# In-chunk key by receptance products made once and kept in DRAM, receptance 0 projected ahead of key 1

## The chip, the cores and the metric

The kernel runs on one core of a Trainium2 chip. The metric is the device time of one launch in microseconds, the median of three runs. The engines are named as the profile names them: PE (TensorE, with PEld for its weight loads), DVE (VectorE), ACT (ScalarE), POOL (GpSimd) and SP (SyncE, which here only issues DMAs).

## The reference, cut to what matters

Two layers, each with four branches that are fed by one projection of the normalised input (1024 prompt tokens and 8 sequences of 16 new tokens, 1152 in all). The change lies in branch A, a recurrence over tokens with a matrix state `s` of 64 x 64 for each of four heads:

```
def step(s, inp):
    r_t, w_t, k_t, v_t, kk_t, a_t = inp
    sa = jnp.einsum('bhij,bhj->bhi', s, -kk_t)
    s = (s * w_t[:, :, None, :] + sa[:, :, :, None] * (kk_t * a_t)[:, :, None, :]
         + v_t[:, :, :, None] * k_t[:, :, None, :])
    return s, jnp.einsum('bhij,bhj->bhi', s, r_t)
```

`r` is called the receptance, `k` the key, `v` the value. The kernel computes it by chunks of 64 tokens: with the decays worked into keys and receptances, all that the tokens of a chunk do to each other is a masked product of keys by receptances, and the part of it that couples the removal keys is a unit-triangular system, which is inverted.

## The kernel before, in words

**Projections.** The input is projected in 24 tiles of 128 features a layer, in the order `F_ORDER` (L35): WDAD (decay and learning rate), K0 and K1 (keys of heads 0, 1 and 2, 3), R0 and R1 (receptances), V0 and V1 (values), then the tiles of the other branches (D0, GD0, D1, GD1, VC0, VC1, U0, GC0, U1, GC1 and so on). `project` (L238) runs a tile over three groups of 384 tokens; a group is 24 matmuls of 128 x 384 into one of two PSUM banks `pj`, and then a sink on ACT and DVE that empties the bank. WDAD and K0 run side by side, group after group. Weights come as pairs of k-tiles by SP, are split in two parts by ACT (L234) and GpSimd (L235), and are asked for two tiles ahead.

**Work beside the projections.** Generators wait in lanes; `tick` (L135) advances the head of each lane by one step. A projection ticks a few times within each group (for most tiles twice, and once more after the sink, so three times a group). Lane "a" is one queue and holds, in this order, `a_elem` for each key group (L417, elementwise work of a key group, five pieces), `systems` (L496), `solve` (L510) and `recurrence` (L699). The program order that comes out is a priority: a planner places the instructions of each engine, and each engine then runs its own list in order.

**Branch A.** `a_elem(i, g)` writes, for heads pair i and token group g, the tile `KB` (scaled removal keys and keys) and the first half of `AR` (scaled removal keys); `receptance(i, ..)` (L479) multiplies the receptances into the second half of `AR` on GpSimd (L482).
- `systems(g)` (L496): for each of the six chunks of a group four products of 64 by 64 (removal keys only) into one PSUM bank, a mask on DVE (L504) into `ns` (two buffers), and a store on ACT's queue (L505) into the DRAM tile `nd` (`nds` for chunks 16 and 17, the new tokens). Two chunks are one step.
- `solve` (L510): SP loads the diagonal blocks of all chunks (L518, L519), DVE inverts them one per partition (L528 and L530, 46 steps of two operations), ACT issues the stores of the inverses into `dd` and `dds` (L536 to L543).
- `prepare(c)` (L550), in three steps: SP loads the chunk's inverse `tt` (L561), four products of 128 by 128 with key and receptance columns, two DVE masks (L570) into `Gm` (tag `gm`, two buffers), transposes of keys and values; products that complete the inverse with the off-diagonal block; the product of `Gm` with the values (L626).
- `advance(c)` (L631), in three steps: `U` from the state and the inverse, the new state, the outputs (L689, which reads `Gm` last). `prepare` of the next chunk runs beside `advance`.
- `split`, `groupnorm` and the gates use the outputs later.

PSUM tiles `b` (four banks) hold the products of `systems`, `prepare` and `advance`. Large SBUF tiles `m` (eight buffers) hold projections, the inverses and the pooling branch's tiles. The order around the change stands at L895 to L922: `systems(g - 1)` is queued after K1's group g, `systems(2)` and `solve` with idle ticks between them after K1; R0, R1, V0, V1, D0 follow; `recurrence` is queued after D0 and runs beside GD0 to U0.

Of the kernel before, what the change touches and what calls it, by code (L numbers as in the profile page):

```python
# [10 lines left out]
F32 = mybir.dt.float32  # L11
# [19 lines left out]
# projection tiles, in the order in which they are streamed  # L31
# [3 lines left out]
F_ORDER = (WDAD, K0, K1, R0, R1, V0, V1, D0, GD0, D1, GD1, VC0, VC1, U0, GC0, U1, GC1,  # L35
           Q0, Q1K, CK, GB0, GB1, GA0, GA1)

# columns of the per-feature vectors
# [4 lines left out]
# constant matrices  # L43
# [5 lines left out]
def tile_trunk(ctx: ExitStack, tc: tile.TileContext, *aps):  # L49
# [34 lines left out]
    def split(src, by, view=lambda t: t):  # L84
        """two exact parts of a tile; by: engines of the copy and of the difference"""
# [9 lines left out]
    def total(out, m, parts, start=True, stop=True):  # L95
        """sums over partitions of a tile in two parts, weighted by small integers"""
        mm(out, m, parts[0], start, False)
        mm(out, m, parts[1], False, stop)
# [16 lines left out]
    # Work that runs beside the large products: lanes of generators, each advanced by one step per tick.  # L115
# [37 lines left out]
    # running input of the layer: 4 tiles of [128, 2, G] per token group, and sums of squares  # L153
# [15 lines left out]
    # sums over partitions: of all, of each half; of the halves of queries  # L169
# [21 lines left out]
    def raw_weights(fi, src):  # L191
        """a whole tile of weights ahead of its splitting"""
        raw[fi] = m_tile(1024).rearrange("p (k t) -> p k t", k=8)
        SY.dma_start(out=raw[fi], in_=src)
# [14 lines left out]
    def recip1p(t):  # L209
        """t <- 1 / (1 + t)"""  # L210
# [11 lines left out]
    def load_weights(n):  # L222
        """weights as two exact parts, in pairs of k-tiles in their order of use"""
# [14 lines left out]
    def project(keys, hi, lo, sinks, ticks=(3,)):  # L238
        """one tile of features, or several of them side by side, group after group of tokens"""
# [58 lines left out]
    # zero at the first token of each chunk (64 tokens; 16 in the last 128 columns)  # L298
# [11 lines left out]
    # rows of the chunks' inverses, zero off the diagonal blocks  # L310
    # (half chunks of 64 rows; the room behind each lets the diagonal blocks lie at equal distances)
# [3 lines left out]
    def whole(t, c, cols):  # L315
        """the two halves of chunk c"""
        return t[2 * c:2 * c + 2, 0:128 * cols].rearrange("x (s t) -> x s t", s=64)

    def diagonal(t, i, n, cols, first=0):
        """the n x n blocks of the halves' matrices: block b of rows at columns first + b n"""  # L320
# [14 lines left out]
    for l in range(L):  # L335
        last_layer = l == L - 1
# [22 lines left out]
        # ================= A: features with token shift =================  # L359
# [57 lines left out]
        def a_elem(i, g, k):  # L417
# [11 lines left out]
            # decay, learning rate, square sums of the removal key  # L429
# [29 lines left out]
            # normalised removal key  # L459
# [4 lines left out]
            # in-context learning rate  # L464
# [14 lines left out]
        def receptance(i, fr):  # L479
            def after(g, zs):  # L480
                ex = AR[i][g][:, :, 1, :]
                Po.tensor_tensor(out=ex, in0=chv(zs), in1=ex, op=ALU.mult)  # L482
            shifted(fr, lambda g: s_tile("gn", 3), after)
# [7 lines left out]
        nd, nds = halves(f"nd{l}", 32, 64), halves(f"nds{l}", 4, 64)  # L491

# [3 lines left out]
        def systems(g):  # L496
            for cl in range(6):
                c = 6 * g + cl
                pn = pb()[:, 0:128].rearrange("p (i t) -> p i t", i=2)
                for h in range(4):  # L500
                    mm(pn[hp(h), h // 2, :], KB[h // 2][g][hp(h), cl, h % 2, :], AR[h // 2][g][hp(h), cl, 0, :])
                ns = chp.tile([128, 2, 64], F32, tag="u0", name=nm("ns"), bufs=2)
                mk = cm[:, C_MP if c < 16 else C_MS, 0:64]
                V.tensor_tensor(out=ns, in0=pn, in1=mk.unsqueeze(1).broadcast_to([128, 2, 64]), op=ALU.mult)  # L504
                A.dma_start(out=whole(nd, c, 64) if c < 16 else whole(nds, c - 16, 64),  # L505
                            in_=ns.rearrange("p i t -> p (i t)"))
# [43 lines left out]
        def prepare(c):  # L550
            """what a chunk needs besides the state, in three steps"""
# [10 lines left out]
            # masked products of the chunk  # L562
            Gm = chp.tile([128, 2, 2, 128], F32, tag="gm", name=nm("gm"), bufs=2)
            for hh in range(2):
                pg = pb()[:, 0:256].rearrange("p (i t) -> p i t", i=2)
                pr = slice(64 * hh, 64 * hh + 64)
                for i in range(2):
                    mm(pg[:, i, :], KB[i][g][pr, cl].rearrange("p a t -> p (a t)"),
                       AR[i][g][pr, cl].rearrange("p a t -> p (a t)"))
                V.tensor_tensor(out=Gm[:, hh], in0=pg,  # L570
                                in1=cm[:, C_MS if samp else C_MP, :].unsqueeze(1).broadcast_to([128, 2, 128]),
                                op=ALU.mult)
            # token-major copies of keys and values
# [13 lines left out]
            # inverse of the chunk's unit-triangular system  # L587
# [965 lines left out]
```

## Time and profile before

| | us |
|---|---|
| three runs | 1474.29, 1471.72, 1472.41 |
| median | 1472.41 |
| span of the profiled execution | 1470.1 |
| PE busy in it | 1395.4 |
| DVE, ACT, POOL busy | 782.2, 751.9, 436.8 |

The profiled execution is one run; its span goes from the first to the last instruction. Busy time of an engine is the union of its instructions; PE's matmuls overlap each other, so a group's busy time is less than its count times the mean. A wait is put down to what came last by semaphores.

### The profile page before, as it was taken

How to read it: one execution, taken by the hardware profiler on the slowest of the kernel's cores; microseconds unless marked ns; L12 is line 12 of the kernel's file. 1: busy time of each engine (PE TensorE's matmuls, PEld its weight loads, DVE VectorE, ACT ScalarE, POOL GpSimd, SP SyncE). 2: the span in 40 equal slices, each digit the busy share in tenths (PEclk: the TensorE clock that was granted, in tenths of full speed). 3: DMA queues.
4: the chain of work that ended last, by engine and by line, in shares of the span. 5: the costliest groups of instructions: out<-in, count | busy, mean ns of one | idle time of the engine just before them, and what ended most of it. 6: DMA issues, size and time to landing. Idle time of an engine off the chain costs nothing. (4 is left out here: it accounts for less than half of the span.)

```text
span 1470.1 us, 26810 instructions
## 1 busy us (share of the span) xinstructions
PE 1395.4 (95%) x9938; PEld 1158.6 (79%) x9938; DVE 782.2 (53%) x1762; ACT 751.9 (51%) x2017; POOL 436.8 (30%) x575
## 2 busy tenths in 40 slices
PE   4898899999999999999979988999999999999999
PEld 3678778888987776689967787888899778666998
DVE  7985944445136457742387857433632464677211
ACT  6672244655366667642257522455644666666210
POOL 4514314346321110322262333332652111112320
PEclk9999999999999999999989999999999999999999
DMA  7113241111212114033300123221021111131232
GB/s 224 48 33 81 52 101 49 55 46 38 93 42 70 53 31 130 6 114 97 87 22 29 52 66 73 77 69 47 30 78 60 57 53 55 37 109 43 69 96 77
DMA packets 116594, 97.38 MB, mean 66 GB/s; under 512 B 46128, under 2 KB 111344, under 8 KB 116464
## 3 DMA queue, kind: packets, MB, share of 16 engines
q1 hardware_dynamic: 76776, 73.74, 17.1%
q10 hardware_dynamic: 39688, 21.94, 5.0%
q8 instruction: 78, 1.28, 0.4%
q14 instruction: 52, 0.43, 0.1%
HBM read 71.48 MB, written 24.16 MB: 65 GB/s over the span
## 5 line engine op out<-in xcount | busy, mean ns | idle before, releaser
L76 PE MATMUL pj<-xh,wh 128*128 128x384 f32 x1152 | 413.6, 360 | 18.5 <-ACT xh L273 7.3
L76 PE MATMUL pj<-xl,wh 128*128 128x384 f32 x1152 | 395.4, 343 | 4.1 <-POOL xl L275 3.1
L76 PE MATMUL pj<-xh,wl 128*128 128x384 f32 x1152 | 394.8, 343 | 0.0
L235 POOL TENSOR_TENSOR wl<-wr,wh 128x256 fp32r<-128x256 f32 x200 | 155.0, 783 | 484.3 <-ACT wh L234 421.9
L76 PEld LDWEIGHTS pj<-xh,wh 128*128 128x128 f32 x1152 | 220.2, 191 | 45.2 <-ACT sho L390 11.5
L76 PEld LDWEIGHTS pj<-xl,wh 128*128 128x128 f32 x1152 | 220.3, 191 | 11.8 <-POOL xl L275 5.5
L76 PEld LDWEIGHTS pj<-xh,wl 128*128 128x128 f32 x1152 | 220.0, 191 | 7.6 <-issue 6.4
L76 PE MATMUL pj<-yh,wh 128*128 128x384 f32 x384 | 130.0, 339 | 2.4 <-DVE x L1376 2.4
L76 PE MATMUL pj<-yh,wl 128*128 128x384 f32 x384 | 129.2, 336 | 0.0
L76 PE MATMUL pj<-yl,wh 128*128 128x384 f32 x384 | 129.0, 336 | 0.0
L234 ACT ACTIVATE wh<-wr 128x256 fp32r<-128x256 f32 x200 | 80.8, 414 | 93.9 <-PE pj L76 45.9
L76 PEld LDWEIGHTS pj<-yh,wh 128*128 128x128 f32 x384 | 72.5, 189 | 3.7 <-DVE x L1376 2.8
L235 POOL TENSOR_TENSOR wl<-m,wh 128x256 fp32r<-128x256 f32 x56 | 43.5, 787 | 102.2 <-ACT wh L234 75.8
L76 PEld LDWEIGHTS pj<-yh,wl 128*128 128x128 f32 x384 | 72.7, 189 | 0.1
L76 PEld LDWEIGHTS pj<-yl,wh 128*128 128x128 f32 x384 | 72.6, 189 | 0.1
L1251 ACT ACTIVATE X<-b,ng 128x512 f32<-128x512 f32 (+3 forms) x96 | 54.9, 575 | 28.8 <-DVE ng L1243 24.7
L76 PEld LDWEIGHTS st<-X,X 128*64 128x64 f32 x576 | 35.7, 136 | 31.7 <-DVE mx L1239 6.3
L76 PE MATMUL b<-sp,cr 128*128 128x384 f32 (+3 forms) x192 | 58.7, 386 | 1.0 <-POOL sp L92 0.6
L1239 DVE TENSOR_REDUCE mx<-b 128x1 f32<-128x512 f32 (+3 forms) x96 | 53.0, 552 | 8.3 <-PE b L76 6.9
L1372 DVE TENSOR_TENSOR pt<-pj,pt 128x384 f32<-128x384 f32 x24 | 13.4, 557 | 80.6 <-PE pj L76 80.6
L234 ACT ACTIVATE wh<-m 128x256 fp32r<-128x256 f32 x56 | 22.5, 413 | 62.0 <-PE pj L76 60.9
L76 PE MATMUL st<-X,X 128*64 128x128 f32 x576 | 53.6, 283 | 0.3
(295 smaller groups left out, 2556.9 us busy)
## 6 DMA issues: line engine op xcount, KB each, us to landing
wr<-in_win_dram SPq DMA_DIRECT2D x176, 128.0 KB
m<-in_wout_dram SPq DMA_DIRECT2D x12, 512.0 KB
x<-in_xT_dram SPq DMA_DIRECT2D x12, 384.0 KB
ysp<-m ACTq DMA_DIRECT2D x24, 192.0 KB
pt<-in_xT_dram SPq DMA_DIRECT2D x24, 192.0 KB
ea<-ysp SPq DMA_DIRECT2D x24, 192.0 KB
x1d<-x ACTq DMA_DIRECT2D x24, 192.0 KB
pt<-x1d SPq DMA_DIRECT2D x24, 192.0 KB
```

Of the source, the lines that this page charges most:

```text
L76: PE.matmul(out, lhsT=lhsT, rhs=rhs, start=start, stop=stop, skip_group_check=True)
L234: A.activation(out=h, in_=r, func=AF.Copy)
L235: Po.tensor_tensor(out=lo, in0=r, in1=h.bitcast(F32), op=ALU.subtract)
L1239: V.tensor_reduce(out=mx[:, b:b + 1], in_=pc[:, :w], axis=AX.X, op=ALU.max)
L1251: A.activation(out=P[:, :w], in_=pc[:, :w], func=AF.Exp, scale=SCALE, bias=ng, accum_out=sums[pr][:, b, s, h:h + 1])
L1372: V.tensor_tensor(out=xr, in0=ps, in1=xr, op=ALU.add)
```

## The change

`F_ORDER` gets R0 between K0 and K1, and the order of the calls follows. `systems(g)` is queued after the receptance of group g of R1 has been multiplied in, makes the four products of 128 by 128 that `prepare` made, masks them into `Gm` (tag `gm`, two buffers), stores the removal-key half to `nd` in two pieces on SP's queue and the whole `Gm` to a new DRAM tile `gd` on ACT's queue. `prepare` loads `Gm` from `gd` on SP's queue in place of products and masks. `solve` follows after two idle ticks.

```diff
-F_ORDER = (WDAD, K0, K1, R0, R1, V0, V1, D0, ...
+F_ORDER = (WDAD, K0, R0, K1, R1, V0, V1, D0, ...
...
         def receptance(i, fr):
             def after(g, zs):
                 ex = AR[i][g][:, :, 1, :]
                 Po.tensor_tensor(out=ex, in0=chv(zs), in1=ex, op=ALU.mult)
+                if i == 1:
+                    go("a", systems(g))
...
         nd, nds = halves(f"nd{l}", 32, 64), halves(f"nds{l}", 4, 64)
+        gd = dr.tile([18, 128, 512], F32, tag=f"gd{l}", name=nm("gd"))
...
         def systems(g):
             for cl in range(6):
                 c = 6 * g + cl
-                pn = pb()[:, 0:128].rearrange("p (i t) -> p i t", i=2)
-                for h in range(4):
-                    mm(pn[hp(h), h // 2, :], KB[h // 2][g][hp(h), cl, h % 2, :], AR[h // 2][g][hp(h), cl, 0, :])
-                ns = chp.tile([128, 2, 64], F32, tag="u0", name=nm("ns"), bufs=2)
-                mk = cm[:, C_MP if c < 16 else C_MS, 0:64]
-                V.tensor_tensor(out=ns, in0=pn, in1=mk.unsqueeze(1).broadcast_to([128, 2, 64]), op=ALU.mult)
-                A.dma_start(out=whole(nd, c, 64) if c < 16 else whole(nds, c - 16, 64),
-                            in_=ns.rearrange("p i t -> p (i t)"))
+                samp = c >= 16
+                pg = [pb()[:, 0:256].rearrange("p (i t) -> p i t", i=2) for _ in range(2)]
+                for i in range(2):
+                    for hh in range(2):
+                        pr = slice(64 * hh, 64 * hh + 64)
+                        mm(pg[hh][:, i, :], KB[i][g][pr, cl].rearrange("p a t -> p (a t)"),
+                           AR[i][g][pr, cl].rearrange("p a t -> p (a t)"))
+                Gm = chp.tile([128, 2, 2, 128], F32, tag="gm", name=nm("gm"), bufs=2)
+                mk = cm[:, C_MS if samp else C_MP, :]
+                for hh in range(2):
+                    V.tensor_tensor(out=Gm[:, hh], in0=pg[hh], in1=mk.unsqueeze(1).broadcast_to([128, 2, 128]),
+                                    op=ALU.mult)
+                for hh in range(2):
+                    half = nds[2 * (c - 16) + hh] if samp else nd[2 * c + hh]
+                    SY.dma_start(out=half[0:128 * 64].rearrange("(s i t) -> s i t", s=64, i=2),
+                                 in_=Gm[64 * hh:64 * hh + 64, hh, :, 0:64])
+                A.dma_start(out=gd[c], in_=Gm.rearrange("p h i t -> p (h i t)"))
                 if cl % 2:
                     yield
...
         def prepare(c):
...
             Gm = chp.tile([128, 2, 2, 128], F32, tag="gm", name=nm("gm"), bufs=2)
-            for hh in range(2):
-                pg = pb()[:, 0:256].rearrange("p (i t) -> p i t", i=2)
-                pr = slice(64 * hh, 64 * hh + 64)
-                for i in range(2):
-                    mm(pg[:, i, :], KB[i][g][pr, cl].rearrange("p a t -> p (a t)"),
-                       AR[i][g][pr, cl].rearrange("p a t -> p (a t)"))
-                V.tensor_tensor(out=Gm[:, hh], in0=pg,
-                                in1=cm[:, C_MS if samp else C_MP, :].unsqueeze(1).broadcast_to([128, 2, 128]),
-                                op=ALU.mult)
+            SY.dma_start(out=Gm.rearrange("p h i t -> p (h i t)"), in_=gd[c])
...
         def after_k1(g, zs):
             start("a", a_elem(1, g, zs))
-            if g > 0:
-                go("a", systems(g - 1))
...
+        receptance(0, R0)
         shifted(K1, lambda g: zk1[:, gcols(g)], after_k1)
-        go("a", idle(4))
-        go("a", systems(2))
-        go("a", idle(4))
+        receptance(1, R1)
+        go("a", idle(2))
         go("a", solve())
-        receptance(0, R0)
-        receptance(1, R1)
         values(V0)
```

## Rows read from the trace of the kernel before

**Rows 1.** The page, part 1: busy us, share of the span, instructions.
```profile
PE 1395.4 (95%) x9938; PEld 1158.6 (79%) x9938; DVE 782.2 (53%) x1762; ACT 751.9 (51%) x2017; POOL 436.8 (30%) x575
```
**Rows 2.** Busy time by stretch: from:to, length, engines, granted clock, DMA share, GB/s.
```profile
97.00:133.00 36.00, 32.60 (x255) 28.28 (x256) 21.58 (x51) 11.95 (x32) 11.84 (x16) 1.00 0.20 56
141.90:186.70 44.80, 39.34 (x273) 36.86 (x272) 42.00 (x118) 9.43 (x28) 16.94 (x24) 0.95 0.22 56
...
205.00:347.00 142.00, 139.63 (x1612) 116.69 (x1611) 62.97 (x144) 80.59 (x278) 59.50 (x75) 1.00 0.18 55
...
38.00:97.00 59.00, 51.71 (x249) 39.55 (x248) 52.68 (x90) 43.94 (x109) 22.53 (x26) 0.96 0.13 37
```
**Rows 3.** Timeline of DVE, masks of `systems`: start, us, what, idle before.
```profile
97.41 0.28 DVE L504 TENSOR_TENSOR ns<-b,cm 128x128 f32<-128x128 f32 x1
...
123.10 0.29 DVE L504 TENSOR_TENSOR ns<-b,cm 128x128 f32<-128x128 f32 x1 [1.58 <-DMA nd<-ns]
...
132.25 0.29 DVE L504 TENSOR_TENSOR ns<-b,cm 128x128 f32<-128x128 f32 x1 [1.53 <-DMA nd<-ns]
```
**Rows 4.** Waits of PE: waited for, us in total, times, longest.
```profile
PE b L76 <- DVE gm L570: 5.9, 3, 2.9
PE b L76 <- DVE ns L504: 5.0, 4, 1.4
```
**Rows 5.** Groups by line and form: shapes, count, busy us, mean ns, idle before.
```profile
L570 DVE TENSOR_TENSOR gm<-b,cm 128x256 f32<-128x256 f32 x72 | 28.3, 417 | 6.7 <-PE b L76 6.7
L76 PE MATMUL b<-ar,kb 64*128 64x128 f32 x288 | 27.0, 302 | 0.0
...
L76 PE MATMUL b<-ar,kb 64*64 64x64 f32 x288 | 15.3, 228 | 5.9 <-DVE ns L504 5.0 <-DVE kb L471 0.8
...
L504 DVE TENSOR_TENSOR ns<-b,cm 128x128 f32<-128x128 f32 x36 | 10.4, 288 | 24.6 <-DMA nd<-ns 21.8 <-PE pj L76 2.3
```
**Rows 6.** Busy time by stretch, as rows 2: stores of `nd`, `dd`, `ysp`.
```profile
121.50:125.50 4.00, 2.71 (x40) 2.13 (x38) 0.61 (x3) 0.00 (x0) 0.77 (x1) 1.00 0.13 36
...
186.90:194.90 8.00, 7.05 (x48) 5.91 (x47) 1.20 (x4) 3.00 (x8) 0.00 (x0) 0.84 0.89 132
196.80:197.40 0.60, 0.60 (x6) 0.60 (x5) 0.60 (x4) 0.48 (x3) 0.01 (x1) 1.00 0.77 277
```
**Rows 7.** Timelines of ACT and SP: two stores and the next issue awaiting each.
```profile
1396.54 0.34 ACTq L1373 DMA_DIRECT2D out_yT_dram<-pt  x1
...
1398.45 0.32 SPq L1370 DMA_DIRECT2D pt<-x1d  x1
...
371.90 0.33 ACTq L891 DMA_DIRECT2D ysp<-m  x1
...
374.73 0.33 SPq L929 DMA_DIRECT2D m<-in_wukv_dram  x1
```
**Rows 8.** The chain that ended last, where projection groups follow each other: start, us.
```profile
1089.32 16.91 PE pj L76 x96
```
**Rows 9.** Timeline of GpSimd: the receptance multiply of R1's first group.
```profile
118.13 1.01 POOL L482 TENSOR_TENSOR ar<-gn,ar 128x384 f32<-128x384 f32 x1 [2.29 <-DVE gn L387]
```
**Rows 10.** Timelines of SP and DVE: a load of the solve, the inversion's first step.
```profile
137.03 0.33 SPq L519 DMA_DIRECT2D m<-nds  x1
...
141.95 0.16 DVE L528 TENSOR_TENSOR m<-m 32x15 f32<-32x15 f32 x1 [0.81 <-POOL wl L235]
```
**Rows 11.** Timeline of PE: waits at the recurrence's start, layers 0 and 1.
```profile
183.40 1.17 PE L76 MATMUL b<-vu,gm 64*64 64x64 f32 x8 [2.92 <-DVE gm L570]
...
916.14 0.45 PE L76 MATMUL b<-cm,m 64*64 64x64 f32 x8 [2.93 <-ACT m L600]
```
**Rows 12.** Busy time by stretch, as rows 2, around the recurrence's start.
```profile
180.00:200.00 20.00, 14.68 (x87) 12.39 (x87) 11.54 (x31) 5.70 (x16) 1.66 (x3) 0.83 0.49 85
```
**Rows 13.** Timeline of PE: a chunk's last read of `Gm`, the next chunk's first.
```profile
221.34 0.40 PE L76 MATMUL b<-gm,vu 128*64 128x64 f32 x8
...
227.51 0.31 PE L76 MATMUL b<-tt,gm 32*32 32x32 f32 x8
```

More of the change, by code (lines that the diff above doesn't have):

```diff
@@ L33 @@
  GB0, GB1, Q0, Q1K, CK, GA0, GA1) = range(NF)
-F_ORDER = (WDAD, K0, K1, R0, R1, V0, V1, D0, GD0, D1, GD1, VC0, VC1, U0, GC0, U1, GC1,
+F_ORDER = (WDAD, K0, R0, K1, R1, V0, V1, D0, GD0, D1, GD1, VC0, VC1, U0, GC0, U1, GC1,
            Q0, Q1K, CK, GB0, GB1, GA0, GA1)
```

## The prediction

> **What bounds the kernel now.** I read the busy totals first: TensorE works 1395.4 of 1470.1 us, the other engines about half of it or less [rows 1]. Where TensorE is that full, a microsecond of its work is worth a microsecond, unless another engine ends a stage; so the table of busy time by stretch comes next [rows 2]. I take layer 0; layer 1 repeats it some 724 us later. In the stretch in which the in-chunk systems are built (97 to 133) TensorE is busy 32.6 of 36 us. In the solve (141.9 to 186.7) VectorE is busy 42.0 of 44.8 us: it is the bound there, and TensorE runs ahead with projections. In the recurrence (205 to 347) TensorE is busy 139.6 of 142 us: what is taken out there is gained whole. The systems have a bound of their own: ahead of a mask `ns` of 0.29 us VectorE idles 1.58 us, until a store of `nd` gives back one of two buffers; 18 chunks take from 97.41 to 132.54, 1.95 us each [rows 3]. Last, what ended TensorE's waits: the masks of `prepare` 5.9 us, those of `systems` 5.0 [rows 4].
>
> **The products.** `systems` now makes four products of 64 keys by 64 columns a chunk, `prepare` four of 128 by 128. The 36 chunks of both layers cost 15.3 us and 27.0 us of TensorE (0.43 and 0.75 a chunk) [rows 5]. The change makes the larger ones once, in `systems`, and drops the smaller. The 27.0 us move out of the recurrence, the 15.3 us vanish: **-15.3 us**. Of the moved work 13.5 us a layer leave a stretch that TensorE bounds, and 5.85 us a layer (13.5 less 7.65) are added to the stretch around R1, where TensorE has little room either; so the net counts, if no new wait arises.
>
> **The masks.** 72 masks of 0.417 us leave the recurrence, 36 of 0.29 us vanish [rows 5]. VectorE isn't the bound of the recurrence, so this gives nothing there. In `systems` it adds 0.83 - 0.29 = 0.54 us a chunk to the loop over the two buffers.
>
> **The stores, the doubtful part.** Each chunk now holds one of two `gm` buffers from its first mask until three stores have landed: 256 KB to `gd` (ACT's queue) and two of 32 KB to `nd` (SP's). The trace shows no such loop, so I bound it. The old `nd` store is slow for its size: in its stretch the DMA engines are 0.13 busy and move 36 GB/s, while a store of 192 KB with 128 rows in its outer dimension uses 0.77 of them at 277 GB/s [rows 6]. The new stores have outer dimensions of 128 and 64, so I take the second rate. From issue to the waiting engine's next step a 192 KB store took 1.9 us undisturbed (1396.54 to 1398.45) and 2.8 us beside a large load (371.90 to 374.73) [rows 7]. For 256 KB, with the issue behind other work of ACT, I add 0.3: 2.2 to 3.1, and take 2.4. A buffer then turns in 0.83 + 0.1 + 2.4 = 3.3 us, and with two buffers a chunk takes 1.67 us (1.57 to 2.0). TensorE's own time there: nine steps of two chunks now follow each other over three projection groups, R1's second to V0's first (by counting the ticks in the code), at 16.91 / 4 = 4.2 us a group [rows 8]: 12.7 + 13.5 = 26.2 us, 1.45 a chunk. So the loop is slower than TensorE by 0.22 us a chunk, 4 us a layer, against 2.5 us now waited for `ns` (5.0 in two layers): **+3 us** for both layers (-1 to +15). What queues behind these waits is why they reach TensorE: on VectorE, behind a waiting mask, the shift sinks of R1 and V0; on ACT, behind the issue of `gd`, the copies out of the two projection banks and of the weights; on SP, behind the two `nd` issues, the weight loads.
>
> The `nd` pieces have rows of 256 bytes. The trace shows what short rows cost: the 128-byte rows of `dd` went at 132 GB/s with the engines 0.89 busy [rows 6]. The Trainium skill (DMA: Bandwidth & Descriptors, Specifications) says that a transfer needs rows of 512 bytes or more for full rate, as smaller ones are read, changed and written back, which speaks against these pieces. The trace agrees as to the rate. By 132 instead of 277 GB/s 64 KB a chunk take 0.26 us more, at most 0.13 a chunk with two buffers, 5 us in all; the sum above leaves that out.
>
> **The later solve.** `systems` of a group now waits for R1's receptance, so it can't start before the multiply on GpSimd that stood at 118.13 [rows 9]; without 9 chunks of small products ahead (3.8 us) that is at about 115. 18 chunks at 1.67 end at 145, against 132.5. From the last mask to the first step of the inversion it now takes 9.4 us (to 141.95), of which the load waits until 137.03 for the last store [rows 10]; with faster stores I take 7.2. The inversion starts at 152 instead of 142 and, 44.7 us long, ends at 197 instead of 186.6. TensorE, 3 us of extra products and 2 of waits later than now, reaches the recurrence at 185.5 (now 183.40 less a wait of 2.92) [rows 11]. So VectorE is 11.5 us behind instead of 6. The two projection groups of GD0 that remain (8.4 us) can fill most of that, since they don't need the recurrence. I count 2 us a layer uncovered: **+4 us** (0 to +18: all 5.5 us a layer, and 3.4 more at the lower clock, below). The recurrence is queued at the same tick as before, and its end has slack: it ends in U0, three projection tiles before the code finishes its lane.
>
> **The waits at the recurrence's start.** `prepare` no longer needs a mask, so the wait of 2.92 us on `gm`, 5.9 us with layer 1's [rows 4], has no cause of its own. But behind it stands the end of the solve: in layer 1 the next wait there is 2.93 us on the copy L600, behind the issues of `dd` on ACT [rows 11]. I count 0 (0 to -5.9). Around this wait, from 180 to 200, the granted clock is 0.83 on the mean, between the levels of 1.2 and 2.4 GHz [rows 12]: 20 x 0.17 = 3.4 us lost, which I take for layer 1 too, and which would go if the waits went.
>
> **The loads.** `prepare` loads 256 KB into `gm` on SP behind `tt`. Its buffer comes free with the output product of the chunk before last (221.34) and is first read at 227.51 [rows 13], 6 us later, about 5.3 with the shorter chunks. A load takes about as long as the store, 2.2 to 3.1 us. It waits in SP's queue, and weight loads queue behind it; these run two tiles ahead, so I count **0** (0 to +32: 1 us for each of 32 chunks).
>
> **Receptance 0 ahead of key 1** puts three light groups between the two stretches of elementwise work that VectorE bears. TensorE idles 59 - 51.7 = 7.3 us from 38 to 97, mostly K0 and K1, in layer 0 [rows 2]; that may take some of it: **-1 us** (-7 to +2). What moves with it are three sinks on ACT and VectorE, three multiplies on GpSimd and the order of two weight tiles on SP; it needs only what K0's elementwise work has left by then.
>
> **Sum:** -15.3 + 3 + 4 + 0 + 0 - 1 = -9.3, from 1470.1 to 1460.8. The three timed runs lie 1.6 to 4.2 us over this span, their median 2.3. So I predict 1463 us, 1455 to 1469 in this case.
>
> **Rivals.**
> (a) Slower: the store loop in `systems` becomes the bound. By itself it eats the whole saving where it costs TensorE 7.65 + 2.5 us a layer, 0.56 us a chunk: from a landing of 3.1 us, just over what the disturbed 192 KB store took. With 3.5 us it costs (4.43 / 2 - 1.45) x 18 = 13.8 us a layer, 11.3 more than now: -15.3 + 22.6 + 4 - 1 = +10, **1483**. For it: weight loads run in the same stretch. Against: DMA engines mostly idle there [rows 6].
> (b) No change: the late solve isn't covered, since D1's tiles need the buffers that the inversion holds. With 5.5 us a layer: -15.3 + 3 + 11 - 1 = -2.3, 1470; with 3.4 more at the lower clock +4.7, 1477; between them **1473**.
> (c) More is won: stores as fast as undisturbed and the start waits gone with their lost clock: -15.3 - 5.9 - 6.8, **1444**.
> (d) Slower: the load of `gm` is late, 1 us a chunk: -9.3 + 32, **1495**. The 6 us of room speak against it.
> The change does what it says, since the products and masks leave `prepare` in the code.
>
> **How the numbers follow.** The forecast has 0.46, (a) 0.18, (b) 0.17, (c) 0.14, (d) 0.05. The range from 1444 to 1483 takes in the forecast, (b), some two thirds of (c) and half of (a): 0.81. A measurement tells 0.2% (2.9 us) from no change. Faster by more: the forecast, (c), and a little of (b): 0.62. Within: most of (b), 0.14. Slower: (a), (d) and the rest of (b), 0.24.
>
> **What would show it.** Products of keys by receptance 128 wide: 288 records of 27 us, all ahead of the solve, none 64 wide. TensorE about 1380 us busy. VectorE's waits ahead of the `gm` mask ended by a store: a chunk every 1.6 to 1.7 us if I am right, over 2 if (a). The first step of the inversion 8 to 12 us later; TensorE's waits at the recurrence's start 5 to 10 us a layer, more if (b). Chunks in the recurrence 0.75 us shorter, with no wait of TensorE on a `gm` load. I am wrong if TensorE's idle time grows by more than 15 us, or if the order of its instructions changes so that projections no longer fill the solve.

## The result

The changed kernel takes **1499.84 us** (median of four runs, 1498.38 to 1500.79), the kernel before 1473.35 us in the same comparison: a ratio of 1.0179, 95% interval 1.0163 to 1.0195. The profiled execution has a span of 1496.6 us against 1470.1. So the change costs 26.5 us, where 9.3 us of gain were forecast; the time lies outside the range.

The page's busy line of after, answering [rows 1]:

```profile
PE 1404.0 (94%) x9650; PEld 1165.5 (78%) x9650; DVE 780.7 (52%) x1726; ACT 752.1 (50%) x2017; POOL 435.3 (29%) x575
```

TensorE is *more* busy than before, though 288 products went. The busy table by stage shows where the time goes. Its stages begin with K0's last group and end where TensorE starts R1's second group, V1's first, GD0's second, VC0's first and GC0's first, in layer 0. First the kernel before (columns: stretch, its length, busy time and count of PE, PEld, DVE, ACT and POOL, granted clock, DMA share, GB/s):

```profile
56.10:117.50 61.40, 54.76 (x319) 42.34 (x317) 53.05 (x101) 39.96 (x101) 18.40 (x25) 0.97 0.15 46
117.50:143.70 26.20, 23.82 (x169) 22.41 (x169) 9.20 (x28) 6.20 (x18) 10.31 (x15) 1.00 0.32 73
143.70:184.50 40.80, 35.34 (x256) 32.86 (x254) 38.46 (x108) 8.81 (x26) 15.72 (x23) 0.98 0.24 58
184.50:261.10 76.60, 74.27 (x799) 62.34 (x799) 32.05 (x72) 38.59 (x131) 24.58 (x35) 0.97 0.30 78
261.10:347.50 86.40, 84.03 (x966) 70.84 (x963) 41.34 (x98) 50.89 (x177) 36.59 (x44) 1.00 0.14 43
```

and the same stages of after:

```profile
57.30:109.00 51.70, 48.74 (x225) 39.95 (x223) 40.71 (x73) 34.14 (x90) 18.80 (x24) 0.93 0.14 44
109.00:153.10 44.10, 40.92 (x260) 32.60 (x261) 28.32 (x63) 10.94 (x29) 9.10 (x12) 1.00 0.45 134
153.10:191.60 38.50, 35.04 (x260) 33.27 (x259) 29.51 (x84) 10.56 (x32) 15.34 (x27) 0.96 0.45 107
191.60:277.50 85.90, 72.59 (x717) 60.48 (x715) 39.08 (x86) 36.14 (x126) 24.70 (x34) 0.88 0.37 94
277.50:360.50 83.00, 79.15 (x901) 67.06 (x900) 35.51 (x81) 51.91 (x178) 36.93 (x45) 1.00 0.24 70
```

The first stage is 9.7 us shorter, the second, with the products, 17.9 longer. The loss comes in the fourth, the start of the recurrence: 13.3 us of it are idle (85.90 less 72.59) against 2.3, and the granted clock is 0.88 against 0.97, a mean between the two levels. That stage has 82 TensorE records fewer and is 9.3 us longer. Over the five stages TensorE's idle time grows from 19.2 to 26.8 us; the lower clock takes 15.5 instead of 4.9 (an estimate: length times one less the granted clock, summed over the stages); the five stages are 11.8 us longer in all, so the work itself falls by some 6. Layer 1 repeats it (from K0's last group to GC0 296.6 instead of 283.8 us). So the idle time and the clock took about three times the work saved.

What comes late is the solve. The copy that ends it, before and after (layers 0 and 1):

```profile
L540 DVE COPY m<-m x2: 1080/1104/1128, 185.6 to 909.4; 128x1024 f32<-128x1024 f32 x2
```

```profile
L553 DVE COPY m<-m x2: 1025/1036/1048, 209.3 to 947.4; 128x1024 f32<-128x1024 f32 x2
```

In layer 0 it comes 23.7 us later. Behind it stand the stores of the inverses in ACT's list (start, duration; the last row is ACT's next work, after 9.93 us idle), and behind these the first prompt chunk on TensorE, at 226.34 (202.89 before), after a wait:

```profile
208.93 0.67 ACTq L555 DMA_DIRECT2D dd<-m  x1
210.32 0.71 ACTq L556 DMA_DIRECT2D dd<-m  x1
211.06 2.29 ACTq L555 DMA_DIRECT2D dd<-m  x1
213.39 3.36 ACTq L556 DMA_DIRECT2D dd<-m  x1
216.80 0.34 ACT L702 ACTIVATE ar<-b 128x64 f32<-128x64 f32 x2 [9.93 <-issue]
```

```profile
226.34 0.43 PE L76 MATMUL b<-tt,gm 32*32 32x32 f32 x8 [3.28 <-issue]
```

From the copy's start to that chunk are 17.1 us, in the kernel before 17.3. This distance holds nearly everywhere: of the 18 kernels in this document, 16 have it between 15.7 and 19.0 us in both layers, wherever the solve ends; the two others are named below. In these 16 the end of the solve sets the start of the prompt's recurrence.

### The profile page after: what moved, and what is told of

Same layout as the page of the kernel before. It is cut to its first block, busy times and chain, and to the rows that moved or that the text cites. A ratio compares the mean times of both kernels' runs of the same rounds, so it can differ in the third digit from the quotient of the medians.

```text
span 1496.6 us, 26417 instructions
## 1 busy us (share of the span) xinstructions
PE 1404.0 (94%) x9650; PEld 1165.5 (78%) x9650; DVE 780.7 (52%) x1726; ACT 752.1 (50%) x2017; POOL 435.3 (29%) x575
## 5 line engine op out<-in xcount | busy, mean ns | idle before, releaser
L76 PE MATMUL pj<-xl,wh 128*128 128x384 f32 x1152 | 401.1, 348 | 2.0 <-POOL xl L275 1.7
L76 PE MATMUL pj<-xh,wl 128*128 128x384 f32 x1152 | 398.8, 346 | 0.0
```

What stands on the lines that cost most here:

```text
L76: PE.matmul(out, lhsT=lhsT, rhs=rhs, start=start, stop=stop, skip_group_check=True)
```

## The experiments

Theory 1: the late solve costs, since TensorE then waits at the recurrence's start and runs at the lower clock behind each wait. Theory 2: the products had to wait for receptance 1 anyway. Theory 3: the loads of `Gm` come late. "Solve" below is the start of that copy in layer 0 (before: 185.6). Times are medians, each with the median of the kernel before on the same chip (1472.5 to 1473.9).

### The late solve alone

The kernel before, with the solve held up:

```diff
+            hold = NT.rearrange("p s t -> p (s t)")
+            for _ in range(16):
+                Po.tensor_copy(out=hold, in_=hold)
```

> The kernel before with 16 copies of the system's tile in place on GpSimd ahead of the inversion (about 1.35 us each, some 22 us a layer), so that the solve ends as late as in the changed kernel; all else as before. Theory 1, the late solve alone is the loss: 10 to 20 us a layer, 1493 to 1513 us, with TensorE at half clock around the start of the recurrence. Rival, the projections cover it as the prediction assumed: under 1480.

Measured: 1513.64 us against 1473.87, 1.0281 (1.0254 to 1.0308). The solve comes 21.9 us later, at 207.5, and 39.8 us are lost, just past the range of theory 1, 19.9 a layer: **0.9 us for each microsecond.** The first prompt chunk starts at 224.63, again 17.1 us behind the copy. TensorE's longest waits from 155 to 262 (us in total, times, longest):

```profile
PE pj L76 <- DVE m L387: 12.7, 1, 12.7
PE b L76 <- DMA tt<-dd: 5.8, 1, 5.8
```

The second is the load of the inverses. The first stands ahead of the recurrence and is of the hold's making: beside GpSimd's copies VectorE's inversion steps take 0.65 to 1.07 us instead of some 0.2, the sink of V0's last group stands behind them in VectorE's list, and TensorE waits for the bank that it empties. The copies, a step beside them and a step after them:

```profile
154.12 6.54 POOL L522 COPY m<-m 128x1024 f32<-128x1024 f32 x6
155.26 1.06 DVE L533 TENSOR_TENSOR m<-m 32x63 f32<-32x63 f32 x1
161.17 0.20 DVE L533 TENSOR_TENSOR m<-m 32x60 f32<-32x60 f32 x1
```

So the edit does more than move the solve, and 0.9 is a price under this hold. That a late solve costs, with none of the change in the kernel, stands: the first prompt chunk comes 21.3 us later, counted from K0's last group, whichever wait fills that time.

### The solve earlier

The kernel before with ten buffers for `ns`:

```diff
-ns = chp.tile([128, 2, 64], F32, tag="u0", name=nm("ns"), bufs=2)
+ns = chp.tile([128, 2, 64], F32, tag=("u0", "kbt", "vu", "tt", "S")[c % 5], name=nm("ns"), bufs=2)
```

> The kernel before with ten buffers for `ns` in place of two (in the tiles of `kbt`, `vu`, `tt` and `S`, which the recurrence uses only later), so that no mask waits for a store; nothing else. The masks of layer 0 should end some 8 to 14 us before 132.5 and the solve as much before 186.6. Theory 1, the solve's end against TensorE's arrival is what counts, on this side too: the wait of 2.92 us on `gm` and the half-clock stretch at the recurrence's start go in both layers and the time falls to 1458 to 1468 us. Rival, before it was early enough: 1471 to 1476.

Measured: **1460.44 us**, 0.9915 (0.990 to 0.993). The solve comes 5.7 us earlier, and 6.0 us a layer are won, about 1 us for each microsecond; but TensorE's waits on these masks, 5.0 us in both layers [rows 4], go as well, and without them the price would be 0.6 (an estimate). No mask waits for a store any more; what ended VectorE's idle time ahead of the masks is TensorE alone (us, times):

```profile
  PE b L76: 8.2, 6
```

```profile
L540 DVE COPY m<-m x2: 1064/1094/1123, 179.9 to 898.4; 128x1024 f32<-128x1024 f32 x2
```

This kernel beats both. Its limit was looked for next, without the idle steps ahead of the solve:

```diff
-        go("a", idle(4))
         go("a", systems(2))
-        go("a", idle(4))
         go("a", solve())
```

> The kernel before with ten buffers for `ns` (1460.4 us) and without the two times four idle steps ahead of the last systems and of the solve, so that the solve's load is issued right behind the last store. Theory 1, each microsecond of the solve's end is worth about one until TensorE no longer waits at the recurrence's start: the inversion starts 5 to 7 us earlier, and the kernel takes 1453 to 1458. Rival, TensorE's arrival is the bound by now: 1459 to 1462.

Measured: 1463.82 us, 0.9929 (0.9915 to 0.9942), no faster, past the rival's range too. The inversion starts at 135.2, no earlier than with the idle steps (135.0), but ends sooner: the copy comes at 176.1 instead of 179.9, and the first prompt chunk only 0.6 us earlier, 21.8 us behind the copy (22.4 in layer 1). From 165 to 260 TensorE has no wait over 0.6 us left, but it needs 62.9 us from K0's last group to R1's second, with the small products crowded in, instead of 59.7. Here TensorE is the bound, as the rival has it, and an earlier solve is worth nothing more.

### The order alone

The kernel before with R0 ahead of K1 in `F_ORDER` and in the calls, nothing else.

> The kernel before with receptance 0 ahead of key 1 and nothing else: systems, stores and prepare as before. Theory 1, the order relaxes VectorE's two elementwise stretches: the 8.4 us by which the changed kernel reached the second group of R1 earlier are the order's, and with the solve at its old place the kernel takes 1457 to 1467 us. Theory 2, those 8.4 us came from the small products and masks that left the stretch of key 1: the order alone gives 1470 to 1475.

Measured: **1487.73 us**, 1.0105 (1.0087 to 1.0124): 13.9 us lost, both expectations missed. The masks start at 105.0 instead of 97.41 [rows 3], the solve comes at 195.4:

```profile
L540 DVE COPY m<-m x2: 1030/1033/1036, 195.4 to 926.8; 128x1024 f32<-128x1024 f32 x2
```

TensorE does win something ahead (V1's first group starts at 139.83 instead of 143.74), but key 1, from which the solve's chain comes, is projected later. 9.8 us later cost 6.9 a layer, 0.7 for one, with what the order wins ahead already taken off.

The other way round, the changed kernel in the old order:

```diff
-        receptance(0, R0)
         shifted(K1, lambda g: zk1[:, gcols(g)], after_k1)
+        receptance(0, R0)
```

> The changed kernel with the old order of projections (K0, K1, R0, R1): products made once, stored and loaded as in the changed kernel. Theory 1a, what the order costs alone (13.9 us) it costs in the changed kernel too, since key 1 and its elementwise work come earlier: 1484 to 1490 us. Theory 1b, the products wait for receptance 1 in either order, so key 1's place doesn't matter: 1496 to 1504, and the solve ends no earlier than in the changed kernel.

Measured: 1499.74 us, as the changed kernel; the solve comes at 208.0. Theory 1b holds: once the systems need receptance 1, key 1's place no longer matters. So the 13.9 us of the order are not a part to be added: order and late products cost by the same end of the solve.

### The store loop

The changed kernel with room for five chunks in `systems`:

```diff
+                tag = ("gm", "tt", "kbt", "vu", "gm")[c % 5]
...
+                    Gh = [chp.tile([128, 2, 128], F32, tag=tag, name=nm("gh"), bufs=2) for _ in range(2)]
```

> The changed kernel, with room for five chunks instead of two in `systems` (two `gm` tiles, and half chunks in the tiles of `tt`, `kbt` and `vu`, which the recurrence uses only later); the chunks in half tiles store `gd` in two pieces. Theory 1, the loop over two buffers and their stores makes the solve late: the steady pair of chunks falls from 3.75 us to about 3.0, the last mask of layer 0 comes at 146 to 149 instead of 154.5, the end of the inversion at 200 to 204 instead of 208.9, and the kernel takes 1480 to 1490 us. Theory 2, the products wait for receptance 1 and for VectorE's own elementwise work, and the loop only fills that time: the last mask moves by less than 2 us and the time stays at 1497 to 1502.

Measured: 1494.24 us, 1.0145 (1.0127 to 1.0163); 5.6 us won. The loop as it is in the changed kernel, VectorE's masks and the issue of the two `nd` pieces of the chunk masked at 140.89:

```profile
140.89 0.76 DVE L513 TENSOR_TENSOR gm<-b,cm 128x256 f32<-128x256 f32 x2 [1.51 <-DMA nd<-gm]
142.38 0.75 DVE L513 TENSOR_TENSOR gm<-b,cm 128x256 f32<-128x256 f32 x2 [0.74 <-DMA nd<-gm]
144.64 0.76 DVE L513 TENSOR_TENSOR gm<-b,cm 128x256 f32<-128x256 f32 x2 [1.50 <-DMA nd<-gm]
```

```profile
141.34 1.16 SPq L517 DMA_DIRECT2D nd<-gm  x2
```

A buffer turns in 144.64 - 140.89 = 3.75 us: the masks, the two issues, which end at 142.50, and 2.14 us until the next mask. It is the two 32 KB pieces that come last, not the 256 KB of `gd`: in layer 0 alone they end 15.4 us of VectorE's idle time ahead of the masks, and `gd` ends none.

```profile
L513 DVE TENSOR_TENSOR gm<-b,cm x36: 410/415/426, 119.5 to 155.3; 128x256 f32<-128x256 f32 x36
...
  DMA nd<-gm: 15.4, 12
```

With five chunks' room 2.7 us of this are left in both layers, the masks of layer 0 end at 147.3 instead of 155.7, the solve comes at 200.3: 9.0 us earlier. Theory 1 is right on the solve, not on the worth of it (2.8 us a layer, 0.3 for one). The other 14.8 us of the delay stay, and theory 2 fits them: the first mask comes at 117.4 even so, instead of 97.41, behind receptance 1. The Trainium skill (DMA: Bandwidth & Descriptors, Anatomy of one DMA) gives a DMA a fixed part of about 2.0 us, most of it the receipt of the last write, for the GpSimd path; the 2.14 us behind an issue on SP, for 32 KB, are near it.

### The loads

The changed kernel with the load replaced by a zero set on GpSimd, by itself and with the inversion cut short, and the short inversion by itself:

```diff
-            SY.dma_start(out=Gm.rearrange("p h i t -> p (h i t)"), in_=gd[c])
+            Po.memset(Gm, 0.0)
```

```diff
-                for s in range(n - 1):
+                for s in range(15 if n == 16 else 16):
```

> The changed kernel without the load of `Gm` in `prepare`: GpSimd sets the tile to zero instead (so the outputs leave out all that the tokens of a chunk do to each other); the products, the stores and the late solve stay. Theory 3, the loads are a part of the loss: the waits on `gm` (7.4 us) and the half-clock stretches behind them go, 1480 to 1488 us. Theory 1 alone, the late solve makes the waits and the loads only show where it ends: 1495 to 1501.

> The changed kernel with the prompt's inversion cut to 16 of its 31 steps (the later steps left out, about half of its 45 us a layer), so that the solve ends about where it ended before. Theory 1, the late end of the solve is what costs: TensorE's waits and half-clock stretches between 195 and 260 go, and the kernel takes 1462 to 1475 us, under the kernel before or near it. Theory 3, the loads of `gm` in the recurrence cost: the waits on them stay, and the time stays over 1488.

> The changed kernel with both suspects out: the prompt's inversion cut to 16 of its 31 steps, and the load of `Gm` replaced by a zero set on GpSimd. Each alone gave little (1490.7 and 1499.6 against 1499.8). Theory 1 with 3, the late solve hides the late loads, and with the solve on time the loads end the waits (4.3 us a layer at the fifth chunk, with a half-clock stretch behind it): both out give 1472 to 1482. Rival, a third thing (TensorE's fixed order around the recurrence's start) costs the rest: 1485 to 1492.

| | solve | us | ratio |
|---|---|---|---|
| changed kernel | 209.3 | 1499.84 | 1.0179 |
| no load | 210.5 | 1499.62 | 1.0168 (1.0131 to 1.0205) |
| short inversion | 192.3 | 1490.73 | 1.0117 (1.0097 to 1.0136) |
| both | 193.1 | 1479.26 | 1.0038 (1.0024 to 1.0051) |

Without the load nothing is won, although 7.4 us of waits on it stood in the trace: other waits take their place (in layer 0 3.5 us on a copy on ACT, 3.3 on GpSimd, 2.0 for the inverses). With the solve 17 us earlier the load is a cost of its own, 11.5 us. The waits on it with the short inversion, in layer 0 from 180 to 262:

```profile
PE b L76 <- DMA gm<-gd: 6.4, 3, 4.3
```

Each of the two hides part of the other: 9.1 us for the short inversion alone, none for the load alone, and of the 26.5 us both together give 20.6. With the loads out the short inversion is worth some 20 us, 0.6 a layer for each microsecond of the solve, with the loads in 0.3. Both kernels still end the solve some 7 us later than the kernel before.

### The most that the products could give

The kernel with ten buffers, without products and masks in `prepare`; once with a 256 KB load of zeros in their place, once with a zero set. First, the same with the old two buffers, as a trial of the load alone, where 18 stores of zeros at the start moved everything by 19.7 us (K0's last group at 75.82 instead of 56.15):

> The kernel before, order, systems, stores and solve unchanged; only `prepare` has no products and masks and loads `Gm` (256 KB, on SP behind `tt`, as in the changed kernel) from a DRAM tile that is filled with zeros at the start, so the products of the chunks are left out. Theory of the prediction, the loads are hidden: the 27.0 us of products go and nothing comes, 1444 to 1450 us. Theory 3, the loads of the first chunks come late whatever the order, behind the weights on SP: 7 us of waits and as much lost to the lower clock as in the changed kernel, 1456 to 1464. With 1 us for each chunk, 1478.

Measured: 1486.25 us, 1.0091 (1.0069 to 1.0114); less the 19.7 us of the start about 1466.6, so 6 of 27 us. Even these can't be put to the products: counted from K0's last group, the solve's copy comes 6.0 us earlier than in the kernel before (199.25 less 75.82 against 185.55 less 56.15), which the edit wasn't meant to do. With ten buffers and one store at the start:

> The kernel before with ten buffers for `ns` (1460.4 us), and in `prepare` the load of a 256 KB tile of zeros from DRAM in place of products and masks, so the chunks' products are left out (13.5 us of TensorE a layer less); the tile is stored once at the start. It is the most that the change could gain: solve early, products gone, one load a chunk. Theory 1 alone: the saving shows once the solve is early, 1434 to 1442. Theory 3, the loads and the wait for the solve take half of it: 1444 to 1452. Rival, the recurrence's start is bound by VectorE's solve still and what leaves TensorE there becomes waiting: 1455 to 1462.

> The kernel with ten buffers for `ns`, products and masks left out of `prepare`, and no load either: GpSimd sets `Gm` to zero (so the chunks' products are left out). Against the one with the load (1463.9 us) it prices the loads where the solve is early. Theory 3, the late load of the fifth chunk and the half-clock stretch behind it cost 6 to 8 us a layer: 1448 to 1453 us. Rival, the wait for the solve and for the new tokens' chunk at the recurrence's start takes the saving whatever comes later: 1459 to 1465.

Measured: with the load 1463.90 us, 0.9936 (0.9921 to 0.9952); without it 1457.06, 0.9901 (0.9884 to 0.9917); with the products 1460.44. So **27 us less work of TensorE give 3.4 us, which these intervals don't tell from nothing, and with the load nothing.** Both times miss the ranges on record, nearest to those of the rivals; the price of the load is clear, 6.8 us between the two. From K0's last group to GC0 in both layers, ten buffers:

```profile
56.50:342.90 286.40, 271.05 (x2499) 230.35 (x2498) 174.89 (x403) 144.03 (x452) 105.51 (x140) 0.98 0.22 58
780.80:1058.90 278.10, 266.38 (x2497) 227.42 (x2496) 166.40 (x390) 140.85 (x444) 102.06 (x137) 0.99 0.22 59
```

and without products and loads:

```profile
57.60:339.70 282.10, 262.31 (x2356) 222.74 (x2356) 162.33 (x366) 143.75 (x451) 113.16 (x156) 0.97 0.23 59
779.80:1053.50 273.70, 255.73 (x2353) 218.42 (x2352) 156.55 (x354) 141.06 (x444) 109.93 (x153) 0.99 0.23 60
```

TensorE is 19.4 us less busy in the two stretches, and they are 8.7 us shorter (the spans differ by 5.0); 10.7 became idle time. The first prompt chunk starts at 198.5 in both: what leaves TensorE ahead of it only lengthens the wait for the solve (5.0 us, on a copy on ACT behind the issue of the inverses). Behind it lie many waits under 1 us, of which none stands out; that part stays open.

With the load, TensorE's one long wait on it in layer 0 is at the fifth chunk, 4.2 us; that the 6.8 us of the load lie there, once a layer, is an inference. The chunk's buffer is free at 222.5; SP's list with the load, then TensorE's step:

```profile
222.46 0.33 SPq L231 DMA_DIRECT2D wr<-in_win_dram  x1
222.88 0.50 SPq L566 DMA_DIRECT2D tt<-dd  x1
223.48 1.06 SPq L231 DMA_DIRECT2D wr<-in_win_dram  x2
224.63 0.38 SPq L568 DMA_DIRECT2D gm<-gd  x1
```

```profile
231.89 0.28 PE L76 MATMUL b<-tt,gm 32*32 32x32 f32 x7 [4.18 <-DMA gm<-gd]
```

It is issued behind three pieces of weights and `tt`, and TensorE's step comes 7.3 us after the issue. In layer 0 no later chunk waits for its load.

### Only half of the products made once

The order and the early systems of the kernel with ten buffers (six here); the removal-key half of all products is made there and stored, the receptance half in `prepare`, and the load goes one chunk ahead. Nothing is left out.

```diff
+                    mm(pn[h % 2][:, h // 2], KB[h // 2][g][hp(h), cl].rearrange("p a t -> p (a t)"),
+                       AR[h // 2][g][hp(h), cl, 0, :])
...
+                mm(pg[h % 2][:, h // 2], KB[h // 2][g][hp(h), cl].rearrange("p a t -> p (a t)"),
+                   AR[h // 2][g][hp(h), cl, 1, :])
```

> A kernel that takes the change's idea without its late solve and its late load: the order before; `systems` makes the removal-key half of all products (four of 128 keys by 64 columns a chunk) and stores it, with as many buffers (six) as the recurrence leaves; `prepare` makes the receptance half only (64 columns) and loads the other half one chunk ahead. TensorE's products fall from 42.3 to about 31 us. If a load with slack and an early solve are what was missing: 1449 to 1456 us. If a saving in `prepare` isn't gained there: 1458 to 1465, the same as with ten buffers alone (1460.4). If the two stores of `nd` on SP make the solve late again: over 1466.

Measured: 1491.81 us, 1.0123 (1.0091 to 1.0155), 31.4 us more than with ten buffers alone. The idea was to keep the early solve, and it didn't: in the profiled execution (1500.66 us, the longest of six) the copy comes 16.0 us later than in the kernel with ten buffers, which by the prices above is most of the loss. The stores aren't the cause, since what ended VectorE's idle time ahead of the masks is TensorE alone:

```profile
195.99 1.13 DVE L546 COPY m<-m 128x1024 f32<-128x1024 f32 x1
  PE b L76: 33.4, 24
```

One premise was wrong besides: half as many columns don't cost half. At full clock, in the recurrence (205 to 358; and 190 to 343 of the ten-buffer kernel):

```profile
L76 PE MATMUL b<-ar,kb 64*128 64x64 f32 x128 | 10.8, 284 | 0.0
```

```profile
L76 PE MATMUL b<-ar,kb 64*128 64x128 f32 x128 | 11.8, 297 | 0.0
```

0.084 us against 0.092. The 64 x 64 products of the old `systems` take 15.3 / 288 = 0.053 [rows 5]. The Trainium skill (TensorEngine Tiling (Array Packing), Tiling Modes) has the array hold four tiles of 64 x 64 at once but two of 64 x 128; the rows agree: with 128 keys the gain of the small products is gone. By these prices the products of this kernel are 6 us more work, not 11 less (an estimate: 576 times 0.084 against 42.3). And where they crowd, from 98 to 119, the granted clock is 0.52 with TensorE busy without a gap, which alone would make the solve some 10 us later (21 times 0.48, an estimate); below it the same stretch of the kernel with ten buffers:

```profile
98.00:119.00 21.00, 21.00 (x77) 15.67 (x78) 9.61 (x25) 6.17 (x14) 1.32 (x3) 0.52 0.23 64
98.00:119.00 21.00, 20.98 (x168) 17.66 (x169) 18.02 (x41) 9.45 (x23) 8.16 (x10) 1.00 0.23 68
```

### The stores of the inverses on ACT

Theory 4: ACT's list stands at the issue of `dd` until the inversion ends, with the copies of the next chunk behind it; so the four stores go to SP.

```diff
-                A.dma_start(out=diagonal(dd, i, 32, 128), in_=DT[64 * i:64 * i + 64])
+                SY.dma_start(out=diagonal(dd, i, 32, 128), in_=DT[64 * i:64 * i + 64])
...
```

> The kernel before with ten buffers for `ns` (1460.4 us), and the four stores of `dd` issued on SP instead of ACT. In the trace with ten buffers ACT idles 13.1 us ahead of its step at 186.17, its list standing at these stores until the inversion ends at 181 and 5 us longer, while the copies of the new tokens' chunk and a gate's sink wait behind them. Theory 4, this convoy on ACT is what holds TensorE at the recurrence's start: its waits there (2.6 and 4.4 us, with half-clock stretches behind) go, 1450 to 1456 us. Rival, weight loads now stand behind the stores on SP and TensorE waits for them: 1460 to 1470.

> The kernel with ten buffers, products and masks left out of `prepare` and `Gm` loaded (1463.9 us), and the stores of `dd` on SP. Theory 4: the wait of 5.0 us a layer at the recurrence's start goes with its lost clock and the saving appears: 1445 to 1453 us. Rival, the recurrence's first chunks wait for the inverses all the same: 1460 to 1466.

> The changed kernel with the stores of `dd` on SP instead of ACT. Theory 4 with 1: the waits on ACT's copies (4.9 us in two layers) and some of the half clock go, the first prompt chunk still comes 16 us behind the solve's end: 1486 to 1495 us. Rival, the solve's end alone sets it: 1497 to 1502.

Measured: 1466.05 us in the kernel with ten buffers, 0.9947 (0.9933 to 0.9961), 5.6 slower than with the stores on ACT; 1460.34 in the one without products (with the load, 1463.90 before), 0.991 (0.989 to 0.993), at the edge of the noise; 1503.49 in the changed one, 1.0208 (1.0181 to 1.0234), past both ranges. Theory 4 falls, since none gains what it forecast: in the first the first prompt chunk starts at 198.35, as with the stores on ACT (198.52), though its copy is 1.9 us later, and waits for the inverses:

```profile
198.35 0.22 PE L76 MATMUL b<-tt,gm 32*32 32x32 f32 x3 [1.17 <-DMA tt<-dd]
```

In the changed kernel that wait is 10.1 us long, and the chunk stands 27.2 us behind the copy (27.7 in layer 1). ACT's list does stand at these issues, but behind them stands the arrival of the inverses.

## Why the prediction was wrong

**The late solve (+4, 0 to +18): the step that failed.** Its place was right, its size not. The inversion's end was put at 197; it came at 210.3, and TensorE met the recurrence at 186.2 (187.69 less a wait of 1.53; 185.5 forecast). Of the 13.3 us, 4.5 are the first mask (119.5; 115 forecast), 6.1 the loop (2.01 us a chunk instead of 1.67, 18 chunks), 1.2 the way from the last mask to the inversion (8.4 us) and 1.5 the inversion itself (46.2). And more stayed uncovered than the 2 us a layer that were to be left when two groups of GD0 have filled the rest. Projections did fill some. From K0's last group to the first prompt chunk, before and after (stretch, length, busy time and count of projection products alone, clock, DMA):

```profile
56.10:202.89 146.79, 102.46 (x521) 0.97 0.25 61
57.30:226.34 169.04, 117.27 (x582) 0.95 0.35 91
```

61 products more are two and a half groups, some 10.7 us at the rate of [rows 8]; but the chunk comes 22.2 us later (24.1 in layer 1, with 62 more), so by this estimate 11.5 and 13 us stay uncovered, some 25 us in both layers where the sum has 4. The hold above, with 16 more, filled far less, which is a reason for its higher price. So there is no one price: the runs that move the solve show 0.3 to 1.05 us a layer for each microsecond, 0.3 where late loads stand behind it, and most of them change something else as well. The wait comes in pieces, and from 185 to 265 of after the granted clock is 0.85; TensorE's waits there are

```profile
PE b L76 <- DMA gm<-gd: 4.4, 2, 2.9
PE b L76 <- DVE m L663: 3.8, 1, 3.8
PE b L76 <- issue: 3.3, 1, 3.3
PE b L76 <- ACT m L605: 1.8, 1, 1.8
PE b L76 <- ACT vu L590: 1.5, 1, 1.5
```

The second is one I hadn't seen: the new tokens' chunk 16 needs VectorE (L663), whose list holds the whole inversion first. Rival (b) named the mechanism and priced it at 5.5 us and 3.4 of clock a layer (its sum with the clock comes to +4.5, not +4.7); over the five stages above it is 7.6 and about 10.6. Rival (d) comes nearest in number, 1495, but by luck: the late load by itself costs nothing in the changed kernel. The prediction's own sign of being wrong, 15 us more of TensorE's idle time, came true: 92.6 us instead of 74.7 over the span.

**The products (-15.3).** The sum took the larger products at their old 27.0 us. Between projections ahead of the solve they take 33.3:

```profile
L76 PE MATMUL b<-ar,kb 64*128 64x128 f32 x288 | 33.3, 298 | 7.1 <-DVE gm L513 5.7 <-POOL ar L482 1.1
```

So 42.3 - 33.3 = 9.0 vanish, not 15.3. Worse, the rule behind it, that the work leaves a stretch bound by TensorE and so counts in full, didn't hold: with ten buffers 27 us less gave 3.4. Ahead of the first prompt chunk the saving only lengthens the wait for the solve; why it counts so little behind it stays open.

**The store loop (+3, -1 to +15).** The cycle was forecast as 3.3 us and is 3.75, since the two `nd` pieces on SP land last; I had sized the landing by `gd`. TensorE's wait on the masks hardly changed (5.7 us against 5.0 for `ns` [rows 4]); the loop's cost is the solve's.

**Short rows.** The prediction named 5 us for the 256-byte rows of `nd` and left them out of its sum. The `nd` pieces do come last; but the cycle shows two issues and a landing, and no run here changes the row length alone, so this stays open.

**The loads (0, 0 to +32).** Right for the changed kernel as it is (no load, no gain), wrong behind it: with the solve 17 us earlier they cost 5.7 us a layer. The six us of room were read from a chunk with nothing ahead of it in SP's queue.

**Receptance 0 first (-1, -7 to +2).** Alone +13.9, outside its bounds. I looked at what TensorE and VectorE do in key 1's stretch and not at what key 1 feeds. In the changed kernel it costs nothing more.

**The masks (0)** were right, as far as the trace shows. **The waits at the recurrence's start (0, 0 to -5.9):** the wait on the mask is gone, but the others listed above stand in its place. **Rival (a)** saw a slow loop, but had its cost on TensorE in the systems' stretch, where there is next to none.

## What to carry to other kernels

Work taken from the busiest engine need not count: look first for the chain that starts the stage, and price each edit by what it does to that chain. A chain on another engine that ends where TensorE begins a dependent loop costs its delay less what independent work the order puts ahead of the loop; count that work in both traces before calling a delay covered. Test such a chain by holding it up and by speeding it up, and look in the trace for what else the hold slows. Of two waits that hide each other, taking away one can show nothing.

## What the runs showed of the hardware

The granted clock was 0.52 over 21 us in which TensorE was busy all the time (98 to 119, above; in layer 1 0.54 from 830 to 850), while the ten-buffer kernel, with the smaller products in the same stretch, was granted 1.00 with 20.98 of 21 us busy. Steps of VectorE that take 0.20 us took 1.06 beside copies on GpSimd (above). Two stores of 32 KB on SP held their buffer longer than the 256 KB store issued beside them on ACT, by what ended VectorE's waits; their issue took 1.16 us for the two, that of a 256 KB load on the same queue 0.38 (above).
